# One planner constant becomes one per phase: the delay from another engine's result to TensorE, in a two-layer DeltaNet and attention trunk

## The chip, the cores and the metric

The kernel runs on one core of one Trainium2 chip. Its time is the device time of one launch in microseconds (us). Five engines matter: TensorE (PE in the profile) makes the products, VectorE (DVE) and ScalarE (ACT) the element-wise work, GpSimd (POOL) a small share of it, and SyncE's queue (SP) issues the transfers from device memory. Each engine executes its own instructions in program order; semaphores hold an instruction until the results that it reads are there.

## The reference, cut to what matters

A trunk of two layers works on 256 latent and 256 context tokens, 1024 features, float32. Layer 0 mixes tokens with a gated DeltaNet, layer 1 with differential attention. Each is followed by a SwiGLU channel mixer, and each sub-layer is modulated by shift, scale and gate from the conditioning vectors and closed with a layer norm.

```python
for i in range(DEPTH):                       # 2 layers
    h  = x   * (1.0 + sc1)  + sh1            # latent tokens
    hc = ctx * (1.0 + sc1c) + sh1c           # context tokens
    y, yc = _gated_deltanet(h, hc, ...) if i == 0 else _diff_attention(h, hc, ...)
    x = _layernorm(ALPHA * x + gt1 * y)
    x = _layernorm(ALPHA * x + gt2 * _swiglu(x * (1.0 + sc2) + sh2))
    ...                                      # ctx alike, but not in the last layer

# DeltaNet, for each of 8 heads and both directions, in chunks of tokens:
a_low = where(strict, (k * beta) @ k.T * gamma, 0)
u, w  = triangular_solve(eye + a_low, [v * beta, k * beta * exp(G)])
v_new = u - w @ s                            # s: the state, 128x128
o     = q_dec @ s + (q @ k.T * gamma) @ v_new
s     = s * exp(g_last) + k_dec.T @ v_new

# attention, for each of 8 heads: two softmax maps
a = softmax(q0 @ k0.T) - lam * softmax(q1 @ k1.T)
o = a @ v
```

## The kernel before

**Tiles.** All 512 tokens stay on chip, as four tiles of 128 tokens (t = 0 to 3). A float32 product is made as three products of rounded parts (`mm3`): high by high, high by low, low by high. In the names, `hh` and `hl` are the high and low part of the activations, `wh` and `wl` those of a weight tile `w` (`wx`, `wxh`, `wxl` alike in a second pool). Weights stream in as pieces of 512 KB. For each, ScalarE casts the high part (`wh<-w`, line 424), and VectorE or GpSimd subtracts it to get the low part (`wl<-w,wh`, line 410), whichever the planner ends sooner on.

**The DeltaNet heads.** A head is nine small programs that wait for one another: decay factors, convolutions and norms of k, q and v, the matrix N of key products, its triangular inverse (`head_inv`), the scan over four chunks in both directions (`head_scan`), the output, and its split into parts. The inverse is built up from blocks of 8 to 16, 32 and 64: each step is two small products on TensorE with a copy on ScalarE or VectorE between them and a subtraction and transposition on VectorE behind. Its names in the profile are the PSUM tiles `wb` and `o`, the operands `t` and `qz`, and `N`. The scan goes round through PSUM tile `wc`, the residual `r`, the result `Y` and `yc`, and the state `SS`.

**Dense work beside it.** The projections of all heads (tile `pj`), the modulation products (`pj<-w,sT`, a 32-row product) and the output projection are one long thread, `dense_run`. It has the last rank, so it fills TensorE wherever no head has anything ready.

**The planner.** Nobody writes the order of instructions down. While the program is built, a list scheduler (`Sched`) simulates all five engines. Every small program is a thread. At each step the scheduler works out for each thread when its next instruction could start: when its engine is free, its operands are there and its PSUM bank is free, plus a planned delay between engines, `lag(frm, to)`. It issues the thread whose start is earliest, with ties by rank, and moves that engine's clock on by the instruction's modelled length. So each engine's program order is the order of planned starts; on the chip nothing of the planned times is left but this order. `lag` takes the delay from a table by the pair of engines (128 to 203 ns), with one exception: into TensorE from any other engine it is `TO_PE`, 300 ns. The delay also stands behind a PSUM bank that another engine used last.

**Products of ones.** Where the plan leaves TensorE idle for 1000 ns or more, `warm` puts as many products of a matrix of ones (line 536) into the gap as fit into its length less 600 ns, at 216 ns each. Their result is not used.

**Phases.** The plan has five phases, started by `go(k)`: 0 the DeltaNet with its projections and the first half of the output projection, 1 the rest of it and the layer norm, 2 the channel mixer of layer 0, 3 the attention with its output projection, 4 the channel mixer of layer 1. `go` also sets two other constants of the planner by phase: `BETA`, how far it lets an instruction of a better rank go ahead, and `LO_WAIT`, a handicap of VectorE where it competes with GpSimd for a low part.

## Time and profile before

| what | us |
|---|---|
| median of 3 runs | 1284.76 (1284.17 to 1285.11) |
| the profiled execution | 1284.39 |
| its span, first to last instruction | 1282.6 |
| TensorE busy in it | 1239.9 |
| VectorE busy | 891.3 |
| ScalarE busy | 575.8 |
| GpSimd busy | 322.5 |

In this execution the DeltaNet with the projections lasts to about 433 us, the rest of the output projection and the layer norm to 496, the first channel mixer to 846, the turn to layer 1 to 874, the attention with its output projection to 1061, its layer norm to 1097, and the second channel mixer to the end. A busy share is a mean over these stages. In the rows of the prediction, a number in brackets at the end of a timeline row is the idle time of that engine ahead of the instruction, with the result that ended it; in the rows of waits the three numbers are the sum in us, the count and the longest.

### The profile page before, as it was taken

What the parts mean: (1) busy time and instruction counts of PE and PEld (TensorE: products, weight loads), DVE (VectorE), ACT (ScalarE), POOL (GpSimd) and SP (SyncE); (2) the same over time, 40 slices, a digit from 0 to 9 for tenths busy, and PEclk for the clock granted to TensorE, in tenths of its full rate; (3) what the DMA queues carried; (4) which work ended last, traced back from release to release, by engine and by line L of the source; (5) the groups of instructions that cost most, each with busy time, mean ns of one, the idle gap of its engine ahead of it and who ended that gap; (6) DMA issues with size and microseconds to landing.
All of it is one profiled execution on the core that took longest, in us unless ns stands there. A gap on an engine that the chain in (4) does not pass through costs nothing.

```text
span 1282.6 us, 24147 instructions
## 1 busy us (share of the span) xinstructions
PE 1239.9 (97%) x9576; PEld 1018.9 (79%) x9576; DVE 891.3 (69%) x2036; ACT 575.8 (45%) x1295; POOL 322.5 (25%) x190
## 2 busy tenths in 40 slices
PE   9999899999999999999999999999999998999997
PEld 6576678788787787888888888879878866999986
DVE  3298859698783776888378562475998978655546
ACT  2258657667644435222112322145545444444431
POOL 0013212123222148222101123134122236322200
PEclk9999999999999999999999999999999999999999
DMA  9423312011111743555256563224223155755550
GB/s 367 150 78 137 133 43 76 19 51 51 35 51 61 252 140 133 196 174 180 97 172 209 189 198 104 81 85 144 91 87 124 53 200 182 237 188 184 181 181 33
DMA packets 54753, 171.58 MB, mean 134 GB/s; under 512 B 5744, under 2 KB 14064, under 8 KB 53872
## 3 DMA queue, kind: packets, MB, share of 16 engines
q1 hardware_dynamic: 54640, 170.04, 39.6%
q8 instruction: 75, 1.23, 0.4%
q14 instruction: 38, 0.31, 0.1%
HBM read 168.97 MB, written 1.05 MB: 133 GB/s over the span
## 4 chain that ended last, share of the span: by engine, by line
PE 77%; DVE 15%; ACT 5%; issue 2%; DMA 0%; DVEq 0%; SPq 0%
PE pj L459 32%; PE wa L459 18%; PE wc L459 11%; PE wb L459 6%; PE o L459 6%; DVE acc L420 2%; DVE sm L416 1%; DVE sm L420 1%; PE pj L536 1%; ACT jk L437 1%; PE wc L463 1%; DVE sm L410 1%; DVE hl L410 1%; DVE wl L410 1%; ACT N L424 1%
## 5 line engine op out<-in xcount | busy, mean ns | idle before, releaser
L424 ACT CAST wh<-w 128x1024 fp32r<-128x1024 f32 (+1 forms) x131 | 136.9, 1046 | 207.5 <-PE wa L459 54.8
L459 PE MATMUL pj<-hl,wh 128*128 128x512 f32 (+1 forms) x592 | 219.3, 371 | 0.0
L459 PE MATMUL pj<-hh,wh 128*128 128x512 f32 (+1 forms) x592 | 218.1, 368 | 0.6 <-DVE acc L420 0.6
L410 POOL TENSOR_TENSOR wl<-w,wh 128x1024 fp32r<-128x1024 f32 (+1 forms) x40 | 97.3, 2432 | 385.7 <-ACT wh L424 337.1
L459 PE MATMUL pj<-hh,wl 128*128 128x512 f32 (+1 forms) x512 | 187.5, 366 | 0.0
L459 PEld LDWEIGHTS pj<-hh,wh 128*128 128x128 f32 x592 | 112.5, 190 | 15.7 <-issue 1.1
L459 PEld LDWEIGHTS pj<-hl,wh 128*128 128x128 f32 x592 | 112.2, 190 | 14.5 <-issue 0.7
L410 DVE TENSOR_TENSOR wl<-w,wh 128x1024 fp32r<-128x1024 f32 x52 | 63.5, 1222 | 64.1 <-ACT wh L424 62.7
L459 PEld LDWEIGHTS pj<-hh,wl 128*128 128x128 f32 x512 | 97.3, 190 | 10.6 <-issue 0.2
L459 PE MATMUL wa<-hl,wh 128*128 128x256 f32 (+2 forms) x288 | 96.5, 335 | 0.0
L459 PE MATMUL wa<-hh,wh 128*128 128x256 f32 (+2 forms) x288 | 96.0, 334 | 0.0
L420 DVE SCALAR_TENSOR_TENSOR adaE<-w,sT,adaE 128x512 f32<-128x512 f32 x89 | 73.2, 859 | 5.3 <-DMA w<-in_adaw_dram 4.7
L424 ACT CAST wh<-wx 128x1024 fp32r<-128x1024 f32 x36 | 37.8, 1049 | 58.0 <-PE pj L459 28.1
L420 DVE SCALAR_TENSOR_TENSOR acc<-pj,cst,acc 128x510 f32<-128x510 f32 (+1 forms) x80 | 59.3, 742 | 5.9 <-ACT acc L437 5.0
L459 PE MATMUL wa<-hh,wxl 128*128 128x512 f32 (+1 forms) x176 | 61.7, 350 | 0.0
L459 PE MATMUL pj<-hh,wxl 128*128 128x512 f32 (+1 forms) x176 | 60.9, 346 | 0.0
L459 PEld LDWEIGHTS wa<-hh,wh 128*128 128x128 f32 (+1 forms) x288 | 54.4, 189 | 6.0
L459 PEld LDWEIGHTS wa<-hl,wh 128*128 128x128 f32 (+1 forms) x288 | 54.0, 188 | 6.0
L410 POOL TENSOR_TENSOR hidl<-w,hidh 128x512 fp32r<-128x512 f32 x20 | 29.2, 1462 | 108.1 <-ACT hidh L424 108.1
L410 POOL TENSOR_TENSOR wxl<-w,wh 128x1024 fp32r<-128x1024 f32 x13 | 31.5, 2428 | 82.1 <-ACT wh L424 50.5
L459 PE MATMUL wa<-hh,wl 128*128 128x256 f32 (+2 forms) x152 | 49.9, 328 | 0.0
L410 POOL TENSOR_TENSOR h1l<-fth,h1h 128x256 fp32r<-128x256 f32 x20 | 29.4, 1472 | 77.8 <-ACT h1h L424 77.8
(664 smaller groups left out, 3242.8 us busy)
## 6 DMA issues: line engine op xcount, KB each, us to landing
w<-in_adaw_dram SPq DMA_DIRECT2D x71, 512.0 KB, 4.2
w<-in_wgu_dram SPq DMA_DIRECT2D x59, 512.0 KB, 4.5
w<-in_wd_dram SPq DMA_DIRECT2D x31, 512.0 KB, 3.8
w<-in_wdn_dram SPq DMA_DIRECT2D x26, 512.0 KB, 3.8
wx<-in_adaw_dram SPq DMA_DIRECT2D x17, 512.0 KB, 3.9
w<-in_wo_dram SPq DMA_DIRECT2D x15, 512.0 KB, 4.9
wx<-in_wgu_dram SPq DMA_DIRECT2D x15, 512.0 KB, 4.2
wx<-in_wd_dram SPq DMA_DIRECT2D x10, 512.0 KB, 3.9
```

The costliest lines, as they stand in the source:

```text
L410: return shared(Op(e, cost(e, o, (a, b)), lambda: E[e].tensor_tensor(o, a, b, op), o, a, b), (a, b))
L416: f = lambda: E[e].tensor_scalar(o, a, s1, s2, o0, o1) if o1 is not None else E[e].tensor_scalar(o, a, s1, s2, o0)
L420: return shared(Op("v", cost("v", o, (a, b), (s,)), lambda: V.scalar_tensor_tensor(o, a, s, b, o0, o1), o, a, b), (a, b))
L424: return Op("s", cost("s", o, (a,)), lambda: S.copy(o, a), o, a)
L437: return Op("s", c, lambda: S.activation(o, a, f, scale=scale, **kw), o, a)
L459: return Op("pe", c, lambda: T.matmul(o, lhsT=l, rhs=r, start=start, stop=stop), o)
L463: return Op("pe", 110.0, lambda: T.transpose(o, a, ident[0:k, 0:k]), o)
L536: T.matmul(t[:, 0:P], lhsT=ones, rhs=ones, start=True, stop=True)
```

## The change

The constant `TO_PE` becomes a tuple with one value for each phase. In phases 0 and 3 it is 500 ns, in the others 300 ns as before. `go(k)` sets it with the phase's other constants. No instruction is written or taken away in the source; the scheduler plans anew, with each hand-over into TensorE 200 ns longer in these two phases. Helper lines move by one in the file after (459 becomes 460, 410 becomes 411, 536 becomes 537).

```diff
--- before.py
+++ after.py
@@ -56,7 +56,7 @@
 
     return ap.unsqueeze(1).to_broadcast([ap.shape[0], n, ap.shape[1]])
 NRAW = 5
-TO_PE = 300.0
+TO_PE = (500.0, 300.0, 300.0, 500.0, 300.0)
 NRAWX = 1
 NW = 10
 NWX = 4
@@ -234,6 +234,7 @@
         self.port = {"v": 0.0, "g": 0.0}
         self.now = 0.0
         self.beta = BETA[0]
+        self.to_pe = TO_PE[0]
         self.warm = None
 
     def spawn(self, gen, rank, time=None):
@@ -247,7 +248,7 @@
             return 0.0
         if frm == "dma":
             return 0.0 if to == "dma" else self.DMA_LAT
-        return TO_PE if to == "pe" and frm != "pe" else self.LAG[frm, to]
+        return self.to_pe if to == "pe" and frm != "pe" else self.LAG[frm, to]
 
     def advance(self, th):
 
@@ -2108,6 +2109,7 @@
     def go(k):
         lo_wait[0] = LO_WAIT[k]
         sched.beta = BETA[k]
+        sched.to_pe = TO_PE[k]
         event("phase", k).time = sched.now
 
     spawn(prep_s(), 1)
```

How this moves TensorE's rows can be read at three places, first of the order before and then of the new one.

The first is TensorE in the inverse of head 0, at the step from blocks of 16 to 32: two small products into tile `wb`, the second of which reads the copy `qz` that ScalarE makes of the first. Between them stand dense products of the projections (`pj`).

```order
L459 MATMUL wb_1440<-t_8_1293,t_3_1073 32x16 x32
L459 MATMUL pj_1388<-hh,wl_1066 128x512
L459 MATMUL pj_1388<-hh,wh_1036 128x512
L459 MATMUL pj_1388<-hl,wh_1036 128x512
L459 MATMUL wb_1440<-t_7_1292,qz_97 32x16 x32
```

The same place in the new order:

```order
L460 MATMUL wb_1434<-t_8_1315,t_3_1082 32x16 x32
L460 MATMUL pj_1289<-hh,wl_1021 128x512
L460 MATMUL pj_1289<-hh,wh_1015 128x512
L460 MATMUL pj_1289<-hl,wh_1015 128x512
L460 MATMUL pj_1289<-hh,wl_1021 128x512
L460 MATMUL pj_1497<-hh,wh_1164 128x512
L460 MATMUL wb_1434<-t_7_1314,qz_97 32x16 x32
```

Three dense products stood between the two; now there are five.

The second is TensorE at the first run of ones, while heads 0 and 1 prepare k and q (`kT`, `qT`) and the modulation products (`pj<-w,sT`) run.

```order
L459 MATMUL wa_994<-qT_541,kT_602 128x128 x4
L536 MATMUL wa_1037<-ones 128x128 x14
L459 MATMUL pj_1030<-w_778,sT 32x512 x2
L459 MATMUL pj_1030<-w_805,sT 32x512 x2
L459 MATMUL pj_1030<-w_837,sT 32x512
L459 MATMUL wa_1058<-kT_697 128x128 x4
```

The same place in the new order:

```order
L537 MATMUL wa_1224<-ones 128x128 x2
L464 MATMUL wa_1220<-cst,kT_1011 128x128 x4
L460 MATMUL pj_1236<-w_1014,sT 32x512 x2
L460 MATMUL pj_1236<-w_1033,sT 32x512 x2
L460 MATMUL pj_1236<-w_1048,sT 32x512 x2
L460 MATMUL pj_1236<-w_1112,sT 32x512 x2
L537 MATMUL wa_1275<-ones 128x128 x2
L464 MATMUL pj_1236<-cst,adaE_1268 128x128 x4
L464 MATMUL wa_1273<-cst,qT_1254 128x128 x4
```

One run of 14 products of ones (each is two passes in the profile, so 28 there) has become two runs of two, with transposes (`cst,kT`, `cst,qT`) and modulation products around them.

The third is TensorE at the end of the DeltaNet. Before, the transposes of the last head (`wb<-cst,on`) stand ahead of the last projection, and a run of ones in front of the output projection (`pj<-wh,hh`).

```order
L459 MATMUL pj_5631<-w_5566,sT 32x512 x2
L459 MATMUL pj_5631<-w_5570,sT 32x512 x2
L459 MATMUL pj_5631<-w_5585,sT 32x512 x2
L536 MATMUL wa_5664<-ones 128x128 x11
L459 MATMUL pj_5650<-wh_5610,hh 128x512
L459 MATMUL pj_5650<-wl_5611,hh 128x512
L459 MATMUL pj_5650<-wh_5610,hl 128x512
```

The same place in the new order:

```order
L460 MATMUL wa_5667<-wl_5513,hh 128x512
L460 MATMUL wa_5667<-wh_5512,hl 128x512
L460 MATMUL wa_5667<-wh_5512,hh 128x512
L464 MATMUL wb_5607<-cst,on_5679 128x128 x4
L460 MATMUL wa_5667<-wl_5513,hh 128x512
L460 MATMUL wa_5667<-wh_5512,hl 128x512
L460 MATMUL wa_5666<-wh_5591,hh 128x512
```

Now the last head's transposes stand among products of the output projection (`wa<-wh,hh` and its like), and no run of ones is in front of these.

On GpSimd, 29 low parts of weight tiles (`wl<-w,wh`, one `wxl`) stand ahead of the first step of the layer norm (`big<-n,lnr`) before, and 33 now. Here are its rows just ahead of that step, first of the order before.

```order
L410 TENSOR_TENSOR wl_5479<-w_5420,wh_5445 128x1024
L410 TENSOR_TENSOR wl_5611<-w_5597,wh_5610 128x1024
L410 TENSOR_TENSOR wl_5642<-w_5636,wh_5641 128x1024
L410 TENSOR_TENSOR wxl_5870<-w_5757,wh_5841 128x1024
L410 TENSOR_TENSOR big_5681<-n_5950,lnr_5682 128x1024
```

The same place in the new order:

```order
L411 TENSOR_TENSOR wl_5603<-w_5590,wh_5602 128x1024
L411 TENSOR_TENSOR wl_5694<-w_5601,wh_5644 128x1024
L411 TENSOR_TENSOR wl_5714<-w_5614,wh_5713 128x1024
L411 TENSOR_TENSOR wl_5769<-w_5707,wh_5762 128x1024
L411 TENSOR_TENSOR wl_5832<-w_5781,wh_5831 128x1024
L411 TENSOR_TENSOR big_5727<-n_5925,lnr_5728 128x1024
```

Two of the heads' products `EG<-EG,qT` stand on GpSimd as well, where before all were on VectorE.

## Prediction

> **What bounds the kernel now.** I read the page first, its span, busy times and chain of waits.

> ```profile
> span 1282.6 us, 24147 instructions
> PE 1239.9 (97%) x9576; PEld 1018.9 (79%) x9576; DVE 891.3 (69%) x2036; ACT 575.8 (45%) x1295; POOL 322.5 (25%) x190
> PE 77%; DVE 15%; ACT 5%; issue 2%; DMA 0%; DVEq 0%; SPq 0%
> ```

> TensorE is the bound: 97% busy, 77% of the chain. The chain leaves it for VectorE and ScalarE in 20% of the span, though both are far from full: there TensorE, which takes its products in program order, stood before a product whose input was late. DMA has no share. Next, the busy times by stretches, to see where this happens.

> ```profile
> 100.00:165.00 65.00, 57.73 (x752) 42.65 (x752) 52.06 (x160) 45.17 (x133) 19.95 (x11) 0.97 0.34 115
> 165.00:230.00 65.00, 63.99 (x1043) 50.48 (x1042) 51.15 (x205) 46.75 (x157) 14.18 (x8) 1.00 0.21 67
> 360.00:433.00 73.00, 72.52 (x782) 56.69 (x783) 45.72 (x126) 32.85 (x86) 18.24 (x8) 1.00 0.29 96
> 496.00:846.00 350.00, 350.00 (x1556) 287.45 (x1555) 221.01 (x306) 90.37 (x113) 75.79 (x40) 1.00 0.48 158
> 874.00:1061.00 187.00, 180.38 (x1143) 150.68 (x1142) 156.78 (x382) 95.90 (x206) 55.55 (x44) 1.00 0.36 122
> ```

> The columns after the length are PE, its weight loads (PEld), DVE, ACT and POOL, then the clock. The first layer's channel mixer (496 to 846) has no gap: nothing can be won there, and its delay stays 300. The DeltaNet stretches show gaps, and DVE at 52 of 65 us; the attention (874 to 1061) misses 6.6 us. The ends of products are modelled, as the page says, so a busy PE can hide short waits. Idle time of the weight loads is a finer gauge; this is what ended it between 100 and 435 us (total, times, longest):

> ```profile
> PEld wb L459 <- ACT t L424: 5.3, 10, 0.9
> PEld o L459 <- ACT t L424: 3.1, 7, 0.7
> PEld wb L459 <- DVE t L410: 2.9, 2, 2.5
> PEld wc L459 <- DVE N L416: 2.6, 5, 1.0
> PEld wc L459 <- ACT Y L424: 1.6, 8, 0.3
> PEld o L459 <- DVE N L416: 1.5, 2, 0.9
> PEld wb L459 <- DVE N L416: 1.1, 2, 0.6
> PEld wb L459 <- ACT qz L424: 0.9, 2, 0.5
> ```

> All eight rows belong to the heads: the triangular inverse (wb, o with t, qz, N) and the scan (wc). They add up to 19.0 us in 38 waits. A typical one, in the timeline of head 7's inverse:

> ```profile
> 393.11 1.05 ACT L424 CAST wh<-w 128x1024 fp32r<-128x1024 f32 x1
> 394.07 0.26 ACT L437 ACTIVATE N<-o 32x128 f32<-32x128 f32 x1
> 394.98 0.30 DVE L416 TENSOR_SCALAR N<-o 32x128 f32<-32x128 f32 x1 [0.34 <-ACT N L437]
> 395.33 0.54 PEld L459 LDWEIGHTS o<-cst,N 64*64 64x64 f32 x16 [0.64 <-DVE N L416]
> ```

> The hand-over itself is short: VectorE ends at 395.28, the weight load starts at 395.33, 0.05 us later. So the planner's 300 ns was no underestimate of it. What is late is the result: ScalarE had a 1.05 us weight cast in front of it. The change buys 200 ns more room against such lateness, per hand-over, at the price that each head's chain is planned longer.

> **The change part by part.** It adds and removes no computation. Its effects, one by one, against the profiled execution's own 1284.39 us (span 1282.6 and 1.8 around it).

> (1) *Waits in the heads.* A wait shrinks by at most 0.2 us where the planner really puts 0.2 us more of other products ahead. Head 0's link shown above has five dense products there instead of three; other links keep theirs, since a product can only be moved behind whole products that are there to take, of 0.23 us each as the chain of waits has them:

> ```profile
> 49.49 5.45 PE pj L459 x24
> ```

> (That is 5.45 over 24.) Ceiling: 38 times 0.2, 7.6 us. Floor: 0, if lateness only shifts. Where waits are mostly 0.2 to 0.7 us long and not every link grows, a bit over half of the ceiling is nearest: 4 us off. Cover: what stands in front are the dense projections, which have to be done anyway; without them the longer plan would be idle time, 0.2 us for each hand-over of the last head.

> (2) *Gaps that the planner saw and filled with products of ones.*

> ```profile
> 114.07 3.29 PE L536 MATMUL wa<-ones 128*128 128x128 f32 x28
> 118.22 1.90 PE L459 MATMUL pj<-w,sT 128*32 128x512 f32 x10 [0.86 <-DVE acc L420]
> 430.29 2.72 PE L536 MATMUL wa<-ones 128*128 128x128 f32 x22
> 432.76 0.48 PE L459 MATMUL pj<-wh,hh 128*128 128x512 f32 x1
> ```

> These two gaps are 4.15 us (114.07 to 118.22) and 2.47 us (430.29 to 432.76). In the new order the first has become two runs of two products of ones, and the second is gone: output-projection products of the earlier heads stand around head 7's last transposes, where before TensorE waited for the last head's result. That work came from behind the gap, so the gain is the gap alone. Ceiling 6.6 us off; floor 0, because gaps under the planner's threshold get no ones and aren't visible as rows. I take 2 us, the smaller gap less a little, and nothing for the first.

> (3) *Attention.* The waits of the matmuls between 840 and 1100 us that the delay reaches:

> ```profile
> PE o L463 <- DVE ao L410: 4.3, 3, 1.8
> PE wa L459 <- DVE qs L410: 1.3, 3, 0.5
> PE wb L459 <- ACT w L437: 0.7, 1, 0.7
> ```

> Seven waits, ceiling 1.4 us, floor 0. The three long ones are not of the kind that 0.2 us cures:

> ```profile
> 1054.80 2.39 POOL L410 TENSOR_TENSOR wxl<-w,wh 128x1024 fp32r<-128x1024 f32 x1 [9.88 <-DVE sm L410]
> 1054.81 2.39 DVE L420 SCALAR_TENSOR_TENSOR sm<-sm 128x2 f32<-128x2 f32 x1
> 1057.23 0.16 DVE L420 SCALAR_TENSOR_TENSOR sm<-sm,sm 128x2 f32<-128x2 f32 x1
> 1058.59 0.41 PE L463 MATMUL o<-cst,ao 128*128 128x128 f32 x2 [1.69 <-DVE ao L410]
> ```

> A two-column VectorE step lasts as long as the GpSimd subtraction that began 0.01 us before it; after it a like step took 0.16. I take 0.8 us off, the other four waits at 0.2 each.

> (4) *GpSimd.* The same happens in the heads:

> ```profile
> 144.22 2.39 POOL L410 TENSOR_TENSOR wl<-w,wh 128x1024 fp32r<-128x1024 f32 x1 [1.24 <-ACT wh L424]
> 144.25 2.38 DVE L410 TENSOR_TENSOR sm<-beta,sm 128x8 f32<-128x8 f32 x1
> 148.47 0.73 PE L459 MATMUL wb<-t,t 32*32 32x16 f32 x64 [2.12 <-DVE t L410]
> L410 POOL TENSOR_TENSOR wl<-w,wh 128x1024 fp32r<-128x1024 f32 (+1 forms) x28 | 68.1, 2432 | 285.4 <-ACT wh L424 249.3 <-PE pj L459 14.0 <-DVE t L410 9.1
> ```

> The last row counts GpSimd's low-half subtractions up to 433 us. In the new order 33 instead of 29 stand ahead of the first layer norm's step on GpSimd, and two of the heads' EG products moved there from VectorE, because the DeltaNet phase is planned to last longer. Six more such steps, and VectorE is rid of four low halves at 1.22 us (not the bound, so 0):

> ```profile
> L410 DVE TENSOR_TENSOR wl<-w,wh 128x1024 fp32r<-128x1024 f32 x52 | 63.5, 1222 | 64.1 <-ACT wh L424 62.7
> ```

> One on GpSimd that meets the chain costs up to 2.2 us (2.38 less the 0.16 of such a step), most meet nothing. Floor 0, ceiling 4 times 2.2, 8.8 us. I take 1.5 us on.
> [...]

> (5) *The end of the DeltaNet.* The last head now ends behind part of the output projection, so gates, loads and layer norm have less dense work beside them. One row, over all its issues, bounds this:

> ```profile
> brow<-in_bgate_dram SPq DMA_DIRECT2D x8, 256.0 KB, 4.2
> ```

> The gate's two halves pass one after the other through one buffer, 4.2 us each to landing. Covered I cost it at nothing, since the first layer norm still stands behind the same output projection; uncovered, one landing, 4.2 us.

> Sum: 1284.39 - 4 - 2 - 0.8 + 1.5 = 1279.1 us. The median of the runs is 0.37 us above the profiled execution, so 1279.5 us.

> **Rivals.**
> *A, no change.* Lateness comes from long steps in VectorE's and ScalarE's queues (the 1.05 us cast, DVE at 52 of 65 us), and a new order only puts it elsewhere: (1) and (3) give nothing, (2) and (4) cancel. For it: waits up to 2.5 us, which 0.2 cannot cover. Against: 36 of the 38 waits above average (19.0 - 2.9) / 36 = 0.45 us. Time: 1284.8 us.

> *B, slower: GpSimd holds VectorE.* Place: the first two heads (around 144 us), where one collision already cost TensorE 2.12 us, and the last two, where the added subtractions stand. Four added collisions on the chain at 2.2 us, less 2 us of (2) and 1 of (1): 1284.8 + 8.8 - 3 = 1290.6 us. It decides from the third collision on, as two (4.4) are paid by the gains. For it: six more steps. Against: of the 28 now there few stop TensorE.

> *C, much faster.* Slack adds up along a head's chain, as a result that is planned later also lets the next step on VectorE be planned later: (1) and (2) near their ceilings. 1284.8 - 7.6 - 5 = 1272.2 us.

> *D, the clock.* The clock is at 0.97 in the first DeltaNet stretch, the one with most idle time, and 1.00 in the other stretches shown. Fewer products of ones could bring a second such dip: (1 - 0.97) times 65 is 2 us. It shifts any of the others by that. [...]

> **How the numbers follow.** Forecast 0.45, A 0.22, B 0.20, C 0.10, D by itself (about 1286.5) 0.03. The forecast's own range, 1274 to 1282, takes (1) from 1 to 7. A measurement of this kernel can tell 0.2%, 2.6 us, from no change, so below 1282.2 is faster. The forecast is so nearly always (0.42) and C is (0.10): 0.52. A, the rest of the forecast and half of D: 0.26. B and the other half: 0.22. For 8 times in 10 the range has to reach into B and C: from 1270 (all ceilings together, 15.6 us, would be 1269) to 1291 (B).

> **What would show it.** (1) holds if the eight rows of waits fall from 19 us towards 15 at unchanged work, and fails if their sum stays. (2): no run of ones near 430 us and no wait in its place. (3): the qs waits fall, the ao ones stay or move with GpSimd. (4): count VectorE steps over 2 us beside a GpSimd step up to 433 us. (5): no new wait on the gates or the layer norm before 496 us. The channel mixers must keep their length (350 us without a gap). I am wrong if the DeltaNet part ends later than now by more than 2 us, and the slow rival has it if the DVE steps held by GpSimd account for that.

## The result, and the profile after

The changed kernel takes 1294.17 us (median of 4 runs, 1291.92 to 1294.53), the kernel before on the same chip 1284.93 us. The ratio is 1.0072 with a 95% interval of 1.0051 to 1.0092: 9.2 us slower. On a second chip it was 1295.67 against 1284.44 us, 1.0088 (1.0069 to 1.0107). The forecast was 5 us faster.

The page of the changed kernel, with its span, busy times and the chain by engine:

```profile
span 1292.5 us, 24062 instructions
PE 1243.0 (96%) x9542; PEld 1018.7 (79%) x9542; DVE 891.7 (69%) x2033; ACT 575.3 (45%) x1297; POOL 330.4 (26%) x191
PE 74%; DVE 18%; ACT 6%; issue 2%; DMA 1%; SPq 0%; DVEq 0%; ACTq 0%
```

The span is 9.9 us longer. No engine has more work worth naming (GpSimd 7.9 us, all others within 3.1), but the chain of waits leaves TensorE more often: VectorE holds 18% of it, where it held 15%.

The busy times by stretches. The columns are as in the prediction; the later stretches are shifted by as much as the same work is later.

```profile
165.00:230.00 65.00, 61.65 (x705) 48.82 (x705) 50.31 (x182) 41.72 (x139) 14.78 (x9) 0.95 0.15 49
360.00:440.00 80.00, 76.93 (x1088) 57.61 (x1087) 47.87 (x145) 36.82 (x108) 13.95 (x6) 1.00 0.24 81
503.60:853.60 350.00, 350.00 (x1559) 287.87 (x1558) 224.06 (x306) 91.06 (x115) 70.52 (x38) 1.00 0.48 160
881.60:1071.60 190.00, 180.81 (x1129) 151.73 (x1128) 157.28 (x386) 91.70 (x197) 53.26 (x41) 0.98 0.35 116
```

The channel mixer is still full. The loss lies ahead of it and in the attention. Three marks in the two timelines say how much: the last transpose of the DeltaNet heads starts at 448.3 us (before 421.6), the last product of the first channel mixer at 866.5 (858.8), the last transpose of the attention at 1069.3 (1058.7). The first says only that the last head is planned later, since dense work goes on around it. By the other two, 7.7 us are lost up to the first channel mixer's end and 2.9 more in the attention.

It doesn't begin as a loss. Count off the products of TensorE as they are done, without those of ones, each at the mean interval to the next that its shape has in the kernel before (an interval over 0.6 us counted as 0.6). The first 100 us of such work are done at 131.3 us, before at 137.9, so the changed kernel is 6.6 us *ahead*, and at 130 us of work, at 167 us, it leads by 9.7. At 200 us of work it is 1.4 ahead, at 350 it is 7.0 behind, and at 380, at 449 us, 7.4. This is what happens in between, at two places in the timeline of the changed kernel:

```profile
239.16 2.37 POOL L411 TENSOR_TENSOR wl<-w,wh 128x1024 fp32r<-128x1024 f32 x1 [7.45 <-ACT wh L425]
239.53 2.08 DVE L411 TENSOR_TENSOR t<-t,t 128x56 f32<-128x56 f32 x1
242.78 0.49 PE L460 MATMUL wc<-v,N 128*128 128x128 f32 x2 [2.02 <-DVE N L417]
...
410.19 2.89 POOL L411 TENSOR_TENSOR wl<-w,wh 128x1024 fp32r<-128x1024 f32 x1 [16.71 <-ACT wh L425]
410.76 2.33 DVE L421 SCALAR_TENSOR_TENSOR sm<-sm,sm 128x4 f32<-128x4 f32 x1
414.09 0.68 PE L460 MATMUL o<-cst,N 64*64 64x64 f32 x16 [1.93 <-DVE N L417]
```

GpSimd starts a low half; VectorE's next step, four columns wide at 410.76, lasts until GpSimd is done, 413.09 against 413.08 us (0.16 us is usual for it, and 0.21 for the step at 239.53); what stands behind it on VectorE, a copy of N for the inverse, is late by as much, and TensorE stands 1.93 us in front of the product that reads N. Five waits of this kind, of 1.5 to 2.2 us, lie at 219, 240, 313, 349 and 412 us, 9.5 us together by the products' starts (each start less that of the product ahead, less the usual interval). Before there was one, 2.3 us at 146 (2.12 in the row that the prediction shows).

The idle time of the weight loads between 100 and 450 us, the eight largest rows that name a result (total, times, longest):

```profile
PEld wc L460 <- DVE N L417: 4.2, 4, 2.2
PEld pj L460 <- DVE acc L421: 3.4, 4, 1.0
PEld o L460 <- DVE N L417: 3.3, 3, 2.4
PEld o L460 <- ACT t L425: 2.7, 5, 0.8
PEld o L460 <- DVE t L1156: 2.3, 1, 2.3
PEld wb L460 <- ACT t L425: 2.1, 6, 0.4
PEld wc L460 <- ACT N L438: 2.0, 1, 2.0
PEld wc L460 <- ACT th L438: 1.7, 2, 0.8
```

The short waits for ScalarE's `t` did shrink, from 8.4 us in 17 to 4.8 us in 11. Fewer and longer waits for VectorE took their place.

### The profile page after: what moved, and what is told of

It is laid out like the page before. It is cut to its first block, busy times and chain, and to the rows that moved or that the text cites. A ratio compares the mean times of both kernels' runs of the same rounds, so it can differ in the third digit from the quotient of the medians.

```text
span 1292.5 us, 24062 instructions
## 1 busy us (share of the span) xinstructions
PE 1243.0 (96%) x9542; PEld 1018.7 (79%) x9542; DVE 891.7 (69%) x2033; ACT 575.3 (45%) x1297; POOL 330.4 (26%) x191
## 3 DMA queue, kind: packets, MB, share of 16 engines
HBM read 168.97 MB, written 1.05 MB: 132 GB/s over the span
## 4 chain that ended last, share of the span: by engine, by line
PE 74%; DVE 18%; ACT 6%; issue 2%; DMA 1%; SPq 0%; DVEq 0%; ACTq 0%
PE pj L460 31%; PE wa L460 18%; PE wc L460 9%; PE wb L460 6%; PE o L460 5%; DVE acc L421 2%; DVE sm L417 2%; PE pj L537 1%; ACT jk L438 1%; DVE t L411 1%; ACT PQ L438 1%; PE wc L464 1%; DVE sm L421 1%; DVE big L421 1%; DVE wxl L411 1%
## 5 line engine op out<-in xcount | busy, mean ns | idle before, releaser
L411 POOL TENSOR_TENSOR wl<-w,wh 128x1024 fp32r<-128x1024 f32 (+1 forms) x48 | 118.1, 2461 | 389.1 <-ACT wh L425 335.1
L460 PE MATMUL pj<-hh,wl 128*128 128x512 f32 (+1 forms) x448 | 170.4, 380 | 0.0
L460 PEld LDWEIGHTS pj<-hh,wl 128*128 128x128 f32 x448 | 85.2, 190 | 12.1 <-issue 0.2
L460 PE MATMUL wa<-hh,wl 128*128 128x256 f32 (+2 forms) x256 | 84.5, 330 | 0.0
L460 PE MATMUL pj<-hh,wxl 128*128 128x256 f32 (+1 forms) x240 | 78.3, 326 | 0.0
L421 DVE SCALAR_TENSOR_TENSOR adaE<-w,sT,adaE 128x512 f32<-128x512 f32 x76 | 61.2, 839 | 5.0 <-DMA w<-in_adaw_dram 4.5
L421 DVE SCALAR_TENSOR_TENSOR acc<-pj,cst,acc 128x508 f32<-128x508 f32 (+1 forms) x80 | 59.4, 743 | 4.5 <-ACT acc L438 3.7
L411 DVE TENSOR_TENSOR wl<-wx,wh 128x1024 fp32r<-128x1024 f32 x28 | 36.0, 1284 | 33.8 <-ACT wh L425 33.7
L411 DVE TENSOR_TENSOR wxl<-w,wh 128x1024 fp32r<-128x1024 f32 x25 | 32.4, 1296 | 30.2 <-ACT wh L425 30.1
L460 PEld LDWEIGHTS wa<-hh,wl 128*128 128x128 f32 (+1 forms) x256 | 48.2, 188 | 4.8
```

The lines of the kernel that those rows point to most:

```text
L411: return shared(Op(e, cost(e, o, (a, b)), lambda: E[e].tensor_tensor(o, a, b, op), o, a, b), (a, b))
L421: return shared(Op("v", cost("v", o, (a, b), (s,)), lambda: V.scalar_tensor_tensor(o, a, s, b, o0, o1), o, a, b), (a, b))
L460: return Op("pe", c, lambda: T.matmul(o, lhsT=l, rhs=r, start=start, stop=stop), o)
```

## Experiments

All times are medians; each run stands beside runs of the kernel before on its own chip.

| run | us | kernel before | difference | ratio, 95% |
|---|---|---|---|---|
| 500 ns, DeltaNet alone | 1288.41 | 1283.65 | +4.8 | 1.0021 to 1.0048 |
| 500 ns, attention alone | 1284.41 | 1283.65 | +0.8 | 0.9983 to 1.0010 |
| 300 ns, GpSimd's low halves in two steps | 1280.32 | 1283.65 | -3.3 | 0.9948 to 0.9976 |
| 500 ns in both, two steps | 1288.84 | 1283.65 | +5.2 | 1.0020 to 1.0051 |
| 300 ns, DeltaNet's low halves left out | 1288.42 | 1285.12 | +3.3 | 1.0012 to 1.0039 |
| 500 ns in DeltaNet, left out | 1279.83 | 1285.12 | -5.3 | 0.9949 to 0.9984 |
| 700 ns, DeltaNet | 1309.53 | 1285.12 | +24.4 | 1.0166 to 1.0216 |
| 200 ns, DeltaNet | 1297.10 | 1285.12 | +12.0 | 1.0075 to 1.0123 |
| 300 ns, left out but for the output projection's | 1280.08 | 1284.47 | -4.4 | 0.9942 to 0.9973 |
| 500 ns in DeltaNet, the same | 1277.92 | 1284.47 | -6.6 | 0.9930 to 0.9974 |
| 290 ns, DeltaNet | 1290.23 | 1284.47 | +5.8 | 1.0022 to 1.0062 |
| 490 ns, DeltaNet | 1284.90 | 1284.47 | +0.4 | 0.9984 to 1.0021 |
| 500 ns in both, again | 1295.67 | 1284.44 | +11.2 | 1.0069 to 1.0107 |
| 300 ns, four steps | 1284.13 | 1284.44 | -0.3 | 0.9974 to 1.0009 |
| 500 ns in DeltaNet, four steps | 1285.87 | 1284.44 | +1.4 | 1.0004 to 1.0032 |
| 490 ns in DeltaNet, four steps | 1280.48 | 1284.44 | -4.0 | 0.9959 to 0.9986 |
| 300 ns, left out in both phases | 1281.57 | 1284.12 | -2.6 | 0.9968 to 0.9994 |
| 500 ns in both, left out in both | 1277.26 | 1284.12 | -6.9 | 0.9934 to 0.9967 |

Theory one: GpSimd's long steps hold VectorE's, and at 500 ns more of them fall where the heads' chain runs. Theory two: the longer plan itself, because each head follows the one before it later (last transposes of heads 2 to 7: 269 to 448 us, before 259 to 422) and dense products are used up early. A third came up on the way: each delay makes another order, and how well it does is a draw.

### The two phases apart

```diff
-TO_PE = (500.0, 300.0, 300.0, 500.0, 300.0)
+TO_PE = (500.0, 300.0, 300.0, 300.0, 300.0)     # and (300.0, 300.0, 300.0, 500.0, 300.0)
```

> 500 ns in the DeltaNet phase alone. In the trace of the changed kernel the last product of the first channel mixer ends 7.6 us later than before and the rest adds 2.3 us, most of it in the attention. If the two phases act by themselves: 1284.9 + 7.6 = 1292.5 us. If the loss hangs on both at once, or on where the attention's work happens to fall, the sum of this run's and the next run's losses differs from 9.2 us by more than 2 us.

> 500 ns in the attention phase alone. If the phases act by themselves: 1284.9 + 2.3 = 1287.2 us, with the DeltaNet part as before. If the attention's loss was only where GpSimd's steps fell after a later DeltaNet, it can come out at no loss, 1284 to 1285 us.

Measured: +4.8 and +0.8 us, together 5.6, not 9.2. The attention alone is no loss that can be told from none. In its trace the attention's last transposes start 6.3 us *earlier* than before (1052.4), and what stands behind, the layer norm, takes that back. The waits there, first of the kernel with 500 ns in the attention alone, then of the kernel before (total, times, longest):

```profile
PE o L464 <- DVE n L417: 3.8, 1, 3.8
PE wb L464 <- DVE n L417: 3.5, 1, 3.5
```

```profile
PE o L463 <- DVE n L416: 4.0, 2, 2.2
```

What ends the chain there is the normalized tile `n`; TensorE came sooner and stood longer, 7.3 us where it had stood 4.0. Behind each of the two waits the clock is low as well (0.57 from 1069 to 1073 us, 0.62 from 1082.5 to 1087, 0.91 over all of 1052.4 to 1090); in the trace of before it is 1.00 there (1061 to 1097 us).

### GpSimd's low halves in two steps

```diff
+        if n >= 1024:                # n: columns of the low half
+            for op in alt:
+                if op.eng == "g":    # one planned step, two instructions
+                    op.fn = lambda: [nc.gpsimd.tensor_tensor(o[:, c:c + n // 2], a[:, c:c + n // 2],
+                                     b[:, c:c + n // 2], ALU.subtract) for c in (0, n // 2)]
```

The order of all other engines is unchanged, row by row.

> The kernel before (300 ns), but each of GpSimd's 128x1024 low-half subtractions is issued as two of 128x512, with every engine's planned order unchanged. Theory one (GpSimd's long steps hold VectorE's steps, and TensorE waits for these): a held step is free after half the time. In the trace of before the waits of this kind on TensorE are 2.3 us at 146, 2.0 at 1044 and 1.9 at 1056; half of them is 3 us: about 1282 us. Theory two (the longer plan itself, the lost cover and the scattered modulation products): no change, 1285 us.

> The changed kernel (500 ns in both phases), with GpSimd's 128x1024 subtractions issued as two of 128x512, with every engine's planned order as in the changed kernel. Theory one: its trace has such waits on TensorE at 219, 240, 313, 349 and 412 us (2.0, 2.2, 1.7, 1.5, 2.1) and in the attention at 957 and 1068 (3.2, 1.4), 14 us together; half of them is 7 us: about 1287 us, so that the loss against the run with 300 ns and halves shrinks from 9 to about 5 us. Theory two: 1294 us, the loss stays at 9 us.

Measured: -3.3 us at 300 ns, as theory one has it. At 500 ns the loss against it stayed at 8.5 us, as theory two has it; but the halves made this kernel faster too, +5.2 us where whole steps gave +9.2 and +11.2, and theory two had no change there. Neither theory gets all of it. The five waits are still there and make 7 us together instead of 9.5. The timeline at 500 ns shows why halving the step is not halving the hold:

```profile
211.57 2.12 DVE L426 COPY t<-N 32x256 f32<-32x256 f32 x2
212.21 2.63 POOL L654 TENSOR_TENSOR wl<-w,wh 128x512 fp32r<-128x512 f32 x2
213.73 1.13 DVE L411 TENSOR_TENSOR sm<-sm 128x4 f32<-128x4 f32 x1
```

The first half holds a copy (2.12 us for two that take 0.28 each by the median of the changed kernel's trace), VectorE gets through, and the second half holds the next step, 1.13 us for four columns that usually take 0.16. TensorE's wait there fell only from 2.0 to 1.9 us. So the length of a step doesn't tell the theories apart; the steps had to go.

### The low halves left out

In place of GpSimd's subtraction, ScalarE's queue issues a copy of the raw weights. The order of TensorE, VectorE and ScalarE stays as it was, row by row.

```diff
+        if sched.first:              # until the first layer norm's phase is planned
+            for op in alt:
+                if op.eng == "g":
+                    op.fn = lambda: nc.scalar.dma_start(o.bitcast(F32), a)
```

> Leaves work out: the low halves that GpSimd makes in the DeltaNet phase are not subtracted; a transfer issued by ScalarE copies the raw weights in their place, so GpSimd has no 2.4 us step there. 300 ns, order of TensorE and VectorE as before. Both theories: faster than before by what the held steps cost there, 2 to 5 us. It is the base of the next run.

> The same left out, with 500 ns in the DeltaNet phase alone. Theory one (the low halves on GpSimd fall on the heads' chain at 500 ns): without them the loss against the run before this one is gone, at most 1 us. Theory two (the plan itself: each head follows the one before it some 3 us later, 446 - 267 us for five heads against 421 - 258, so dense products are used up early and the stage behind has less cover): the loss stays at 5 to 8 us.

Measured: +3.3 and -5.3 us. The second is what theory one said for the pair; the first has a wait that the experiment itself put there:

```profile
435.12 0.80 PE L460 MATMUL pj<-wl,hh 128*128 128x512 f32 x1 [5.56 <-DMA wl<-w]
```

A copy for the output projection landed late. The pair was repeated with those pieces kept on GpSimd:

```diff
-        if sched.first:
+        if kind in ("ab", "st", "dn", "z"):
```

> Leaves work out like the earlier pair: GpSimd's low halves of the DeltaNet's own weights are a copy by a transfer that ScalarE issues. Those of the output projection stay on GpSimd, because in the earlier run at 300 ns TensorE waited 5.8 us at 429 for such a copy, a loss of the experiment's own making. 300 ns. Expected: as that run up to 380 us (3.7 us ahead of before) and nothing lost after, so about 1281.5 us where before is 1285.1.

> The same at 500 ns in the DeltaNet phase. Theory one (held steps): within 2 us of the run before this one, or ahead of it. Theory two (the longer plan by itself): 5 us behind it.

Measured: -4.4 and -6.6 us. Without GpSimd's low halves 500 ns is 2.2 us ahead of 300 ns by the medians (the two intervals overlap, so the lead itself isn't sure); with them it is 4.8 behind. Of the five waits not one is left. The place of 410 us, in the run at 500 ns:

```profile
399.99 0.15 DVE L422 SCALAR_TENSOR_TENSOR sm<-sm 128x4 f32<-128x4 f32 x1
400.72 0.15 DVE L422 SCALAR_TENSOR_TENSOR sm<-sm,sm 128x4 f32<-128x4 f32 x1
402.05 0.68 PE L461 MATMUL o<-cst,N 64*64 64x64 f32 x16
```

The step that took 2.33 us takes 0.15, and TensorE's product has no wait in front of it. Theory one holds for the DeltaNet, and theory two falls as the cause of the loss: the heads still end late (436 us against 419), with no loss. A part of theory two is left. Counted off as above, this run leads the kernel before by 10.7 us at 130 us of work and by 4.6 at 380; with the low halves on GpSimd (500 ns in the DeltaNet alone) 10.4 ahead become 5.0 behind. The difference between the two, 9.3 us, is about the five waits' 9.5. The other 6 us of the early lead go in the later heads without GpSimd's low halves.

### Other delays

```diff
-TO_PE = (500.0, 300.0, 300.0, 500.0, 300.0)
+TO_PE = (700.0, 300.0, 300.0, 300.0, 300.0)     # and 200.0, 290.0, 490.0
```

> 700 ns in the DeltaNet phase alone. Theory two: the heads move apart by as much again, the last one ends some 20 to 25 us later than at 500 ns, and the loss doubles: 8 to 12 us over the kernel before. Theory one: the loss hangs on where GpSimd's steps happen to fall, with no trend in the delay: anything from 2 us faster to 8 us slower.

> 200 ns in the DeltaNet phase alone. Theory two: heads closer together by 1.5 us each, so 0 to 4 us faster than before, as far as more waits for late results don't take it back. Theory one: no trend, from 2 us faster to 5 us slower.

> 290 ns in the DeltaNet phase: a delay 10 ns shorter, but the scheduler plans another order (some 1,270 of TensorE's 5,760 rows stand elsewhere). Theory two, a cost of the delay as such, with 200 ns at 12 us, 300 at 0 and 500 at 5: within 1.5 us of the kernel before. Theory three, each order is a draw in which GpSimd's steps, fragments and gaps fall anew, and 300 ns is a good draw: 3 to 10 us slower than before.

> 490 ns in the DeltaNet phase. Theory two: within 2 us of the run with 500 ns there, 5 us over the kernel before. Theory three: anything from 0 to 15 us over it.

Measured: +24.4 at 700, +12.0 at 200, +5.8 at 290, +0.4 us at 490. Theory two is wrong on all four: it had 200 ns faster, 290 level, 490 like 500, and 700 at half of what it lost. Theory one, which had at most 5 us of loss at 200 ns and 8 at 700, misses both of these. A step of 10 ns moves the time by 5.8 us at one end and by 4.4 at the other, about as much as 200 ns do. That is theory three. Whether a longer delay has a cost beside the draw can't be told from six values; 700 ns, far outside both theories, may hold one.

A bad draw need not be a collision. At 200 ns 8.1 of the 12 us are lost by 100 us of work, and the largest wait there stands beside a VectorE that is busy without a break and a GpSimd that does nothing. The row of 11 us around it (PE, PEld, DVE, ACT, POOL, clock), and the product that waited:

```profile
120.00:131.00 11.00, 6.42 (x48) 4.95 (x47) 11.00 (x36) 3.79 (x12) 0.00 (x0) 0.78 0.14 48
```

```profile
128.93 1.09 PE L464 MATMUL wa<-cst,qT 128*128 128x128 f32 x4 [3.86 <-DVE t L411]
```

For the losses at 200, 290 and 700 ns the low halves were not left out, so how much of them is held steps is open.

### Both phases again, and shorter steps

```diff
-                    ... (o[:, c:c + n // 2], a[:, c:c + n // 2], b[:, c:c + n // 2]) for c in (0, n // 2)
+                    ... (o[:, c:c + 256], a[:, c:c + 256], b[:, c:c + 256]) for c in range(0, n, 256)
```

> The changed kernel itself, 500 ns in both phases, beside the kernel before on this chip. If the two phases add up: 4.8 + 0.8 = 5.6 us over the kernel before. If they interact, as in the first measurement: 9 us over it.

> The kernel before, with each 128x1024 low half on GpSimd issued as four steps of 128x256, order of the other engines as before. Halves gave 3.3 us, leaving the steps out of the DeltaNet 4.4. If the length of a step sets the hold: 4 to 5 us faster than before. If VectorE is held again and again by the next quarter: 3 us or less, as with halves.

> 500 ns in the DeltaNet phase alone, with four steps of 128x256. It lost 4.8 us with whole steps and was 6.5 us faster than before without the steps. If the length of a step sets the hold, three quarters of these 11 us come back: 3 us faster than before. If repeated holds matter, it stays at 0 to 3 us slower.

> 490 ns in the DeltaNet phase alone, with four steps of 128x256. With whole steps it was level with the kernel before (0.4 us slower). If the length of a step sets the hold: 4 to 7 us faster than before, since its trace shows holds of 1.5 to 2.6 us before TensorE at 309, 348 and 410 us. If repeated holds matter: 2 us faster or less.

Both phases together cost 11.2 us again: they don't add. The scheduler carries its clocks from one phase into the next, so 500 ns in the attention behind another DeltaNet is another order. In its DeltaNet the changed kernel has the order of the run with 500 ns there alone, so up to 866 us the two differ by the execution only, of which the clock is a part (0.95 against 1.00 from 165 to 230 us; rival D below). In the order of the attention that came out, a held step falls on the attention's chain; this is the changed kernel's timeline:

```profile
958.26 2.34 POOL L411 TENSOR_TENSOR wl<-w,wh 128x1024 fp32r<-128x1024 f32 x1
958.32 2.56 DVE L411 TENSOR_TENSOR qs<-qr,qs 64x256 fp32r<-64x256 f32 x1
961.03 0.47 PE L460 MATMUL wa<-ks,qs 128*128 128x512 f32 x1 [3.10 <-DVE qs L411]
```

The other fourteen steps of this kind in the trace take 0.42 us each.

Quarter steps gave -0.3 us at 300 ns, less than halves. In the trace they shift the loss: GpSimd, which now has four steps where it had one, is late with the low half itself. The timeline at 300 ns (this execution took 1289.35 us, the longest of its ten, and has 13.7 us at half clock behind 161 us and the lowest clock of the ten, 0.989, so it shows the kind of the loss and not its size):

```profile
435.38 7.62 POOL L653 TENSOR_TENSOR wl<-w,wh 128x256 fp32r<-128x256 f32 x6
443.05 0.50 PE L459 MATMUL pj<-wl,hh 128*128 128x512 f32 x1 [2.37 <-POOL wl L653]
```

Six quarters take 7.62 us, 1.27 each, as long as a half did (2.63 / 2); the median of all quarters in this run is 0.74. At 500 ns they bring 3.4 us of the 4.8 back (+1.4), at 490 ns 4.4 (-4.0). So the hold's length matters, and so do repeated holds. The orders of 300 ns with halves (-3.3) and of 490 ns with quarters (-4.0) are faster than both kernels.

### The low halves left out in both phases

```diff
-        if kind in ("ab", "st", "dn", "z"):
+        if kind in ("ab", "st", "dn", "z") or sched.att:     # sched.att: while phase 3 is planned
```

> Leaves work out: GpSimd's low halves of the DeltaNet's own weights and all those of the attention phase are a copy by a transfer that ScalarE issues. 300 ns, order of TensorE and VectorE as in the kernel before. Expected: the 4.4 us of the run with the DeltaNet's left out, and 2 to 4 us more from the two waits of 2 us at 1044 and 1056, so 6 to 8 us faster than before, unless a copy lands late, which would show as TensorE waiting for a transfer.

> The same with the changed kernel's 500 ns in both phases. If the whole loss is held steps: within 2 us of the run before this one, on either side. If the attention loses by its plan: 3 to 6 us behind it.

Measured: -2.6 and -6.9 us. At 300 ns it is less than expected, and less than with the DeltaNet's alone left out. TensorE waited once for a copy that came late in either run, 2.3 us at 300 ns and 5.5 at 500, so the pair understates both, the second more. Even so 500 ns in both phases is 4.3 us ahead of 300 ns. With the low halves on GpSimd it is 9 to 11 behind. So without GpSimd's low halves nothing is left of the loss of the change, in either phase: it is held steps and what follows from them.

## Why the prediction was wrong

The step that failed is part (4), the cost of GpSimd. It was worked out from the count of subtractions: four more and two other products, most meeting nothing, 1.5 us. The count was the wrong measure. Up to 435 us GpSimd has 26 steps over 2 us in the changed kernel and 27 before. What changed is where they fall. Of VectorE's steps up to there 17 overlap one of GpSimd's and last over 0.5 us longer than the lower quartile of their like, by 26.6 us in all; before 13 and 19.3 us. Of VectorE's steps over 2 us beside one of GpSimd's, which the prediction asked to count up to 433 us, there are 8, before 4. Five reach TensorE where one did. By the runs, GpSimd's low halves in the DeltaNet cost 4.4 us at 300 ns and 4.8 + 6.6 = 11.4 at 500, so the term should have been 7 us for the DeltaNet. For both phases it is 2.6 against 11.2 + 6.9 = 18.1, some 15 us where 1.5 was taken (differences against the kernel before, each on its own chip). The rest of the sum came out smaller than forecast but on its side: without the low halves 500 ns in both phases is 4.3 us ahead of 300 ns, where (1) to (3) have 6.8.

Why the planner doesn't see it is in the code. `start` keeps a step of VectorE that the code marks with `op.port` out of GpSimd's planned time (`self.port`), so no such pair overlaps in the plan. On the chip only the order within each engine and the semaphores are left, and none orders a low half against a neighbour on VectorE that it has no data in common with. With every new plan the pairs fall anew. This is read from the code and the timelines; a plan with such an order enforced was not tried.

Point by point:

(1) *Waits in the heads.* Its own sign came true: the eight rows named make 15.3 us where they made 19.0, and of them the rows for `t` fell by 3.6. The sign was too narrow. Rows that it didn't name grew, as those for `acc` from 1.0 to 3.4 us, for the transposed `t` (L1156) from nothing to 2.3 and for ScalarE's `N` from 0.2 to 2.0. All rows of weight loads that wait for ScalarE or VectorE make 28.3 us before and 33.9 after, in about the same stretch; with the low halves left out they are 27.0 at 300 ns and 27.6 at 500. So without the held steps the term is 0, its floor: lateness only shifts, as rival A said.

(2) *Gaps with products of ones.* Under-sized. Nothing was taken for the first gap, and it is the larger gain: 6.6 us at 100 us of work, and 7.5 in the run with 500 ns in the DeltaNet alone, more than the gap's own 4.15. This lead isn't kept, as said above. The gap near 430 us is gone too, as said. But a small term was missed. Where the modulation products stand together, they start together by the records (four at 159.55 to 159.57 us, four more at 160.00 to 160.02), and a short run takes as long as a longer one. In the changed kernel's timeline:

```profile
159.55 1.06 PE L460 MATMUL pj<-w,sT 128*32 128x512 f32 x8
162.69 1.04 PE L460 MATMUL pj<-w,sT 128*32 128x512 f32 x2
164.09 1.04 PE L460 MATMUL pj<-w,sT 128*32 128x512 f32 x2
```

Runs of two take 1.04 us, a run of eight 1.06 (a count of two is one product). Before, two such runs of two stand between 50 us and the end of the DeltaNet, now seven. Against them, runs of four and ten have become fuller ones: all these runs together take 17.1 us before and 19.2 now, 2.1 us more. This was read from the traces, not tried.

(3) *Attention.* Wrong by its interplay with the phase ahead. The waits for `qs` were to fall from 1.3 us; they are 4.2, of which one held step makes 3.1. Without the held steps they don't fall either: with the low halves left out in both phases they are 1.0 at 300 ns and 1.5 at 500. Alone the delay moved the time by nothing that can be told from noise, since the layer norm behind took the gain.

(5) *The end of the DeltaNet.* Right: between 449 us and the channel mixer's end the two kernels keep their distance (7.4 and 7.7 us).

*The rivals.* B, GpSimd holds VectorE, had the mechanism right and its price nearly so, 2.2 us a piece where 1.5 to 2.2 were measured, and came to 1290.6 us. That it also had the number of pieces, four more, is luck: it took them from added steps, and up to 435 us there are none. It had a chance of 0.20, because few of the 28 subtractions before stopped TensorE. That was the error of judgement: the order before is one draw, and its low count says little of the next. Its places were partly wrong; the waits are in heads 2, 4, 5 and 7, not in the first two and the last two. The prediction's last sign points to B: the DeltaNet part ends over 2 us later, and held steps account for most of it (9.3 us of waits and what they shift, against a clock dip of 2.4). D, the clock, adds to it. The stretch behind the wait at 219 us, in the changed kernel, and the same work in the run with 500 ns in the DeltaNet alone:

```profile
221.00:229.00 8.00, 7.75 (x154) 5.77 (x158) 7.36 (x30) 3.81 (x11) 0.00 (x0) 0.57 0.02 6
```

```profile
218.00:230.00 12.00, 9.48 (x225) 6.96 (x224) 9.50 (x35) 6.48 (x20) 2.76 (x2) 1.00 0.16 46
```

The order there is the same, with the same wait of 2.0 us; in one execution the clock is at half for 6.8 us behind it, in the other not. At 380 us of work the one without is 5.0 us behind the kernel before, the other 7.4. The changed kernel's execution on the second chip has a clock of 0.991 over its span, as on the first (0.995 in the run with 500 ns in the DeltaNet alone), and is 6.1 behind.

The range, 1270 to 1291, ended at B's four pieces less 3 us of gains, and left out that holds in the attention and dips of the clock come on top.

## What to carry to other kernels

This list scheduler keeps a step of VectorE and one of GpSimd that would hold it (2.33 us beside a low half, 0.15 without it) apart only in planned time. The order that is left on the chip doesn't, so a change of any constant draws the collisions anew, and a forecast of a re-planned order needs the spread of such draws (here 10 ns moved 4 to 6 us) more than the sum of its effects. To learn what collisions cost, take the long steps out of the one engine and keep every other engine's order; in this kernel that turned a loss of 9 to 11 us into a gain of 4 over the other delay. Then shorten the held step before tuning delays, and look whether the engine that is shortened gets late itself: halves helped at both delays, quarters at 300 ns did not. And choose a sign that covers all waits of an engine: the eight rows that the prediction watched fell as it said, while the kernel got slower.

## What the hardware showed

*A second step holds again.* By the traces a held step of VectorE ends with the GpSimd step beside it: at 410 us in the changed kernel the one ran to 413.09 us (2.33 us), the other to 413.08 (2.89 us). What the runs add is the alternation: a step cut in two holds twice (2.12 us for two copies beside the first half, 1.13 us for four columns beside the second), and of steps of 128x256 beside three low halves on VectorE (1.74 to 1.76 us each, 1.22 on the mean in the trace of before), six took 1.27 us each where 0.74 is their median.
